# An encoder block on one core: five pairs of blocks by seven products, and accumulating transfers into the residual

## The chip, the cores and the metric

The kernel runs on one core of a Trainium2 chip. The metric is the device time of one execution in microseconds (us); the time before is 1480.17 us, the median of three runs (1477.66 to 1481.79). The core has a matrix engine (TensorE; PE in the profile, its weight loads PEld), a vector engine (DVE), a scalar engine (ACT), GpSimd (POOL) and a queue engine (SP). Each engine works through its own instructions in order; an instruction that waits for another engine or for a transfer holds up everything behind it on its engine. SBUF is the on-chip memory, PSUM holds what TensorE accumulates.

## The reference

One layer of an encoder, 256 tokens by 2048 features, all in 32-bit floats. In the names of the reference (`x` is the residual):

```python
h = rms_norm(x, attn_norm)
qa, ka, va, qb, kb, vb, ga, gb = split(h @ w_in)          # attention in two branches, with a bias table
ya, yb = windowed_gqa(qa, ka, va, ...), dilated_attention(qb, kb, vb, ...)
x = x + (sigmoid(ga) * (ya @ w_branch_a) + sigmoid(gb) * (yb @ w_branch_b)) @ w_out
hf = rms_norm(x, ffn_norm)
g = dwconv_centred(hf @ w_ffn_gate, conv_w, conv_b)
x = x + (gelu(g) * (hf @ w_ffn_up)) @ w_ffn_down          # 2048 -> 5632 -> 2048
x = x + sigmoid(rms_norm(x, ple_norm) @ w_ple_gate) * (p @ w_ple_proj)
return rms_norm(x, final_norm)
```

## The kernel before

**Weights.** All matrices stream through once, cut into 128x128 blocks; a piece is 16 blocks (1 MB), loaded by SP into one of three `raw` buffers (line 198), the next load being asked for when a buffer is free. Each matrix product is made of three 32-bit-rounded ones: a weight is split into a high part `whi` (ACT, line 217) and the rest `wlo` (DVE, line 218), an activation likewise; then high by high, high by low and low by high are added in PSUM. A split takes 8 blocks (1024 columns) as a rule. There are four buffers for splits (`bufs=4`), so that ACT can begin a split when TensorE has ended the one four before it.

**The list of jobs** (`_plan`, line 62) fixes the order: queries, keys and values with attention between them; the gates `ga`, `gb` and the branch products `ba`, `bb` for each quarter of the features; `o` (w_out); then twice 22 chunks of `g` and `u` (gate and up, half of the 44 feature chunks) followed by two down jobs (`d0`, then `d1`, each for the left and the right half of the 2048 output columns); then `pp` and `pg` (the embedding's projection and gate, four quarters each). Work that is due inside a job is hung on a step of it with `at((job, step), ...)`, and a scheduler makes each engine's final order of it.

**The down jobs** (`seven_product`, line 288) take 22 feature blocks as 11 pairs. A plain pair costs eight products of 128 tokens by 512 columns: `p2`, `p3`, `p4`, `c22` twice. A saved pair (numbers below `SAVED`, line 113) takes seven, after Strassen and Winograd: sums of weight blocks are made by DVE in `combine` (line 222: one subtraction of 1024 columns into a scratch tile, line 229, called t13 here; two of 512, lines 233 and 234), and the sums of activations have been made in `add_up` (line 704). A saved pair is split in four parts (1024, 1024, 1024 and 512 columns) that serve two, two, two and one products. `ORDER` (line 112) has the saved and the plain pairs take turns: 4 0 5 1 6 2 7 3 8 9 10. After the last saved pair `spread_sums` (line 721) adds the four extra sums `p1`, `p5`, `p6`, `p7` to the residual `res` with one ACT copy and eight DVE adds; at the end of the job `joined` (line 772) adds `p2`, `p3`, `p4`, `c22` with one DVE add each and, in `d1`, has ACT square the sum (line 781) for the next norm.

**Transposes.** `merge` (line 761) and `flip` (line 740) turn 256 features at a time with four TensorE transposes into a PSUM tile `pt` (two buffers); ACT and DVE then write both halves of the result (lines 367 and 368). In the right down job of `d1` the same two `pt` buffers hold `p6` and `p7`.

**The end.** `pg` multiplies, `gate` (line 783) makes the sigmoid, adds to the residual and has ACT square it; `finish` (line 795) sums the squares (line 798), takes the root on GpSimd (lines 387 and 389), scales and stores. The last gain is a 1 MB load (line 876) on ACT's queue.

Of the kernel before, what the change touches and what calls it, by code (L numbers as in the profile page):

```python
# [16 lines left out]
P = 128  # L17
# [94 lines left out]
ORDER = [4, 0, 5, 1, 6, 2, 7, 3, 8, 9, 10]  # L112
SAVED = 4
# [44 lines left out]
def _encoder(ctx: ExitStack, tc, xt, pt, cols, table, onehot, mask, ident_in, last_gain, wts, xrows, out):  # L158
# [63 lines left out]
    def combine(b, part):  # L222

        if part == 0:
            state["turn"] = turn = 1 - state.get("turn", 1)
            state["t"] = held["spare"][:, turn * PIECE * P:(turn + 1) * PIECE * P].rearrange("p (b n) -> p b n", n=P)
            four = b.rearrange("p (q b) n -> p q (b n)", q=4)
            t13 = state["t"][:, :8, :].rearrange("p (q b) n -> p q (b n)", q=2)
            nc.vector.tensor_tensor(t13, four[:, 1::2], four[:, :2], op=ALU.subtract)
            return b[:, 8:, :]  # L230
        if part == 1:
            t1, t2, t4 = (state["t"][:, c:c + 4, :] for c in (0, 8, 12))
            nc.vector.tensor_tensor(t2, b[:, 12:, :], t1, op=ALU.subtract)
            nc.vector.tensor_tensor(t4, b[:, 8:12, :], t2, op=ALU.subtract)
            return state["t"][:, :8, :]
        return state["t"][:, 8:, :] if part == 2 else b[:, :4, :]
# [200 lines left out]
    hba = big.tile([P, QH, AW], F32, name="hba", tag="b0", bufs=1)  # L437
    hbb = big.tile([P, BH, BW], F32, name="hbb", tag="b1", bufs=1)
# [62 lines left out]
    def bias(h0, n):  # L501

        if h0 < QH:
            dst, lines = hba[:, h0:h0 + n, :], [[1, P]]
# [25 lines left out]
    def scores(heads, y):  # L530
# [17 lines left out]
        a, step = (hba[:, h, :], P) if n == 1 else (hbb[:, h - QH, :], 1)  # L548
# [75 lines left out]
    def after(job, i, acc, u=None):  # L624
# [66 lines left out]
        elif kind == "u":  # L691
            u = gather(acc)
            nc.vector.scalar_tensor_tensor(u, u, 0.5, rt[1], op0=ALU.mult, op1=ALU.mult)
            f = n % FHALF
            v = held["a32"][:, f, :] if f < 2 * SAVED else u
            nc.vector.tensor_tensor(v, u, held.pop(("gelu", n)), op=ALU.mult)
            halves(held["act"][:, f, :], v)
            if f == 2 * SAVED - 1:
                add_up()
# [4 lines left out]
    def add_up():  # L704

        a = held["a32"].rearrange("p (m e) (t n) -> p m e t n", e=2, t=2)
        a11, a12, a21, a22 = a[:, :, 0, 0], a[:, :, 1, 0], a[:, :, 0, 1], a[:, :, 1, 1]
        s = held["s32"]
# [4 lines left out]
        hi, lo = held["shl"][:, 0], held["shl"][:, 1]  # L713
        for c in (slice(0, 2), slice(2, 4)):
            nc.scalar.activation(hi[:, c], s[:, c], AF.Copy)
            nc.vector.tensor_tensor(lo[:, c], s[:, c], hi[:, c].bitcast(F32), op=ALU.subtract)
# [3 lines left out]

    def spread_sums(n, bank):

        q = [[res[:, t, (2 * n + c) * W4:(2 * n + c + 1) * W4] for c in range(2)] for t in range(2)]
        u = held["ff"].tile([P, W4], F32, name="sq4")
        v = held["ff"].tile([P, W4], F32, name="gate", bufs=2)

        def add(dst, a, b):
            nc.vector.tensor_tensor(dst, a, b, op=ALU.add)

        nc.scalar.activation(u, bank["p1"], AF.Copy)  # L730
        add(q[0][0], u, q[0][0])
        add(u, bank["p6"], u)
        add(v, bank["p7"], u)
        add(u, bank["p5"], u)
        add(q[1][0], v, q[1][0])
        add(v, bank["p5"], v)
        add(q[0][1], u, q[0][1])
        add(q[1][1], v, q[1][1])
# [22 lines left out]
    def merge(n, e, m):  # L761
# [6 lines left out]
        hi, lo = (held["merged"][k // SUB][:, k % SUB:k % SUB + 2, c:c + T] for c in (0, T))  # L768
# [3 lines left out]
    def joined(n, t, acc, scale, parts):  # L772

        r = res[:, t, n * W4:(n + 1) * W4]
        if scale == 1.0:
            nc.vector.tensor_tensor(r, acc, r, op=ALU.add)
        else:
            nc.vector.scalar_tensor_tensor(r, acc, scale, r, op0=ALU.mult, op1=ALU.add)
        if parts is not None:
            q = held["ff"].tile([P, W4], F32, name="sq4")  # L780
            nc.scalar.activation(q, r, AF.Square, accum_out=parts[:, t, n:n + 1])

    def gate(n, t, acc, last):

        r = res[:, t, n * W4:(n + 1) * W4]
        u = held["ff"].tile([P, W4], F32, name="gate", bufs=2)
# [3 lines left out]
        q = held["ff"].tile([P, W4], F32, name="sq4")  # L790
        nc.scalar.activation(q, r, AF.Square, accum_out=held["ss3"][:, t, n:n + 1])  # L791
        nc.vector.tensor_tensor(u if last else r, r, held["lg"][:, n * W4:(n + 1) * W4], op=ALU.mult)
        return u

    def finish(t, tail):

        s = sc.tile([P, 2], F32, name="sum")[:, :1]
        nc.vector.tensor_reduce(s, held["ss3"][:, t, :], axis=AX.X, op=ALU.add)  # L798
        r = root(s, 1)
# [11 lines left out]
    def fetch(t, c):  # L811
# [9 lines left out]
        "o": lambda k: held["merged"][k // SUB][:, k % SUB, :], "ba": lambda k: yab[:, k, :],  # L821
# [5 lines left out]
    for i, job in enumerate(_JOBS):  # L827
# [4 lines left out]
        if kind == "gb" and n == 0:  # L832
            held["merged"] = [big.tile([P, SUB, 2 * T], FR, name="merged", tag=a, bufs=1) for a in ("b0", "b1")]
# [8 lines left out]
        if kind == "g" and n == 0:  # L842
            spare = held["spare"] = big.tile([P, KC * T], F32, name="spare", tag="b0", bufs=1)
            held["a32"] = spare[:, :2 * SAVED * T].rearrange("p (k t) -> p k t", t=T)
            held["s32"] = spare[:, 2 * SAVED * T:4 * SAVED * T].rearrange("p (e m n) -> p e m n", e=4, n=P)
# [3 lines left out]
        if kind == "d1" and n == 0:  # L849
            held["pl"] = big.tile([P, KC, 2 * T], FR, name="mov", bufs=1)  # L850
            pr = ff.tile([P, 2, T], F32, name="pr")
# [9 lines left out]
        if kind == "bb":  # L861
            for e in range(2):
                at((i + 1, 3 + 3 * e), merge, n, e, held["m"])
        if kind == "o":
            for e, j in enumerate(((i + 1, 2), (i + 1, 4)) if n < QUARTERS - 1 else ((i + 1, 9), (i + 1, 11))):
                at(j, flip, 4 * n + 2 * e, held["hf"], 1)
        if kind == "d1":
            for e, j in enumerate(((i + 2, 0), (i + 3, 0), (i + 3, 1), (i + 4, 1)) if n else
                                  [(i + 1, k) for k in (17, 18, 19, 20)]):
                at(j, flip, 8 * n + 2 * e, held["pl"], 2)  # L870
        if kind == "pp" and n == 0:
            end = ff.tile([P, 3 * QUARTERS, W4], F32, name="end", tag="act")
            held["ph"] = end[:, :2 * QUARTERS].rearrange("p (t n) w -> p t n w", t=2)
            held["lg"] = end[:, 2 * QUARTERS:].rearrange("p n w -> p (n w)")
        if kind == "pp" and n == 2:
# [47 lines left out]
        elif kind in ("d0", "d1"):  # L923
            for name, t, c in (("p2", 0, 0), ("p3", 0, 1), ("p4", 1, 0), ("c22", 1, 1)):
                joined(2 * n + c, t, acc[name], 1.0, held["ss2"] if kind == "d1" else None)
        elif kind == "pg":
            for t in range(2):
# [3 lines left out]
                if last:  # L931
                    finish(t, tail)
        else:
# [50 lines left out]
```

## Time and profile before

| | |
|---|---|
| runs before | 1481.79, 1480.17, 1477.66 us |
| profiled execution, its own time | 1477.88 us |
| span from the first to the last instruction | 1476.1 us |
| mean granted TensorE clock | 0.997 |
| DVE busy, ACT busy | 1065.5 us (72%), 760.5 us (52%) |
| all transfers | 282.88 MB, mean 192 GB/s; the weights' queue takes 50.8% of the DMA engines' time |

In a timeline row stand start, duration, engine, line, operation, `out<-in` by tile names, shape and count; in square brackets the idle time of the engine before it and who ended it. In rows of the view by lines stand count, busy time, mean duration in ns, idle time before. Matmuls overlap: the step from one start to the next is what one costs.

### The profile page before, as it was taken

To read this page: it belongs to the slowest core of one execution; us is meant where nothing else is said; L and a number is where in the kernel's file an instruction comes from. 1 tells how busy PE (TensorE), PEld (TensorE's weight loads), DVE (VectorE), ACT (ScalarE), POOL (GpSimd) and SP (SyncE) were. 2 spreads that over 40 slices of the span, in tenths; PEclk is the share of its full clock that TensorE was granted. 3 is DMA by queue.
4 is the path that set the end of the run, shared out by engine and by line. 5 is a ranking of instruction groups with operands and counts; after the bars stand their busy time and mean duration, and the time that the engine had idled before them with its cause. 6 is when DMAs were issued, how large, how long until landed. Compare 5 with 4: busy or idle time off the path is not lost. (4 is left out here: it accounts for less than half of the span.)

```text
span 1476.1 us, 19530 instructions
## 1 busy us (share of the span) xinstructions
PE 1462.2 (99%) x7570; PEld 1248.4 (85%) x7570; DVE 1065.5 (72%) x1530; ACT 760.5 (52%) x1072; POOL 3.7 (0%) x9
## 2 busy tenths in 40 slices
PE   9999999999999999999999999999999999999997
PEld 8888888888888888888888888888888888888886
DVE  7686664664554555568898888887889888898565
ACT  7465444444444444555555555554555555655643
POOL 0000000000000000000000000000000000000000
PEclk9999999999999999999999999999999999999998
DMA  9644444445555554545455454555455454555552
GB/s 321 245 156 171 169 171 171 171 177 194 204 197 192 202 207 180 198 171 197 178 196 196 180 196 171 205 223 192 183 196 189 184 198 172 201 200 216 211 188 97
DMA packets 46375, 282.88 MB, mean 192 GB/s; under 512 B 5124, under 2 KB 9988, under 8 KB 14028
## 3 DMA queue, kind: packets, MB, share of 16 engines
q1 hardware_dynamic: 44268, 277.31, 50.8%
q10 hardware_dynamic: 2016, 4.33, 1.1%
q8 instruction: 59, 0.97, 0.2%
q14 instruction: 32, 0.26, 0.0%
HBM read 279.49 MB, written 2.14 MB: 191 GB/s over the span
## 5 line engine op out<-in xcount | busy, mean ns | idle before, releaser
L218 DVE TENSOR_TENSOR wlo<-raw,whi 128x1024 fp32r<-128x1024 f32 (+2 forms) x519 | 622.1, 1201 | 355.6 <-ACT whi L217 352.4
L217 ACT ACTIVATE whi<-raw 128x1024 fp32r<-128x1024 f32 (+2 forms) x519 | 541.1, 1043 | 605.5 <-PE acc L269 224.9
L244 PE MATMUL acc<-mov,whi 128*128 128x512 f32 x1840 | 641.9, 393 | 0.3 <-DVE mov L368 0.3
L245 PE MATMUL acc<-mov,wlo 128*128 128x256 f32 x1840 | 512.8, 279 | 0.0
L244 PEld LDWEIGHTS acc<-mov,whi 128*128 128x128 f32 x1840 | 344.7, 187 | 77.6 <-DVE mov L368 0.6
L245 PEld LDWEIGHTS acc<-mov,wlo 128*128 128x128 f32 x1840 | 346.7, 188 | 0.4
L268 PE MATMUL acc<-wlo,mov 128*128 128x512 f32 (+1 forms) x512 | 196.5, 384 | 0.5 <-DVE wlo L218 0.5
L267 PE MATMUL acc<-whi,mov 128*128 128x512 f32 (+1 forms) x512 | 196.8, 385 | 0.0
L269 PE MATMUL acc<-whi,mov 128*128 128x512 f32 (+1 forms) x512 | 196.4, 384 | 0.0
L267 PEld LDWEIGHTS acc<-whi,mov 128*128 128x128 f32 x512 | 96.7, 189 | 19.3 <-DVE wlo L218 0.8
L268 PEld LDWEIGHTS acc<-wlo,mov 128*128 128x128 f32 x512 | 96.7, 189 | 19.0 <-DVE wlo L218 0.9
L269 PEld LDWEIGHTS acc<-whi,mov 128*128 128x128 f32 x512 | 96.7, 189 | 18.8
L312 PE MATMUL acc<-wlo,act 128*128 128x512 f32 x272 | 106.3, 391 | 0.8 <-DVE wlo L218 0.8
L311 PE MATMUL acc<-whi,act 128*128 128x512 f32 x272 | 106.1, 390 | 0.0
L313 PE MATMUL acc<-whi,act 128*128 128x512 f32 x272 | 105.9, 389 | 0.0
L312 PEld LDWEIGHTS acc<-wlo,act 128*128 128x128 f32 x272 | 51.1, 188 | 12.0 <-DVE wlo L218 1.7
L311 PEld LDWEIGHTS acc<-whi,act 128*128 128x128 f32 x272 | 51.1, 188 | 10.7
L313 PEld LDWEIGHTS acc<-whi,act 128*128 128x128 f32 x272 | 51.1, 188 | 10.5
L267 PE MATMUL acc<-whi,merged 128*128 128x512 f32 x128 | 50.6, 396 | 0.0
L269 PE MATMUL acc<-whi,merged 128*128 128x512 f32 x128 | 49.9, 390 | 0.0
L268 PE MATMUL acc<-wlo,merged 128*128 128x512 f32 x128 | 49.8, 389 | 0.0
L217 ACT ACTIVATE whi<-spare 128x1024 fp32r<-128x1024 f32 x32 | 33.7, 1054 | 27.0 <-PE acc L313 26.2
(177 smaller groups left out, 1373.0 us busy)
## 6 DMA issues: line engine op xcount, KB each, us to landing
raw<-in_wts SPq DMA_DIRECT2D x251, 1024.0 KB, 4.8
raw<-in_wts SPq DMA_DIRECT2D x12, 512.0 KB, 7.4
x<-in_xrows ACTq DMA_DIRECT2D x8, 256.0 KB, 5.3
x<-in_xt SPq DMA_DIRECT2D x13, 128.0 KB, 6.6
hbb<-hold SPq DMA_DIRECT2D x3, 514.0 KB, 6.3
hba<-hold SPq DMA_DIRECT2D x2, 768.0 KB, 7.1
end<-in_last_gain ACTq DMA_DIRECT2D x1, 1024.0 KB, 4.8
out<-x ACTq DMA_DIRECT2D x2, 384.0 KB
```

What stands on the lines that cost most here:

```text
L217: nc.scalar.activation(hi, src, AF.Copy)
L218: nc.vector.tensor_tensor(lo, src, hi.bitcast(F32), op=ALU.subtract)
L244: nc.tensor.matmul(acc, hi[:, o, :], m, start=first, stop=False, skip_group_check=True)
L245: nc.tensor.matmul(acc[:, T:], lo[:, o, :], m[:, :T], start=False, stop=last, skip_group_check=True)
L267: nc.tensor.matmul(acc, xh, hi, start=(k == 0), stop=False)
L268: nc.tensor.matmul(acc, xh, lo, start=False, stop=False)
L269: nc.tensor.matmul(acc, xl, hi, start=False, stop=(k == n - 1))
L311: nc.tensor.matmul(acc, xh, hi, start=(e == 1), stop=False)
L312: nc.tensor.matmul(acc, xh, lo, start=False, stop=False)
L313: nc.tensor.matmul(acc, xl, hi, start=False, stop=(e == uses[name]))
```

## The change

- `SAVED` goes from 4 to 5 and the order of pairs becomes 5 0 6 1 7 2 8 3 4 9 10: saved pairs 3 and 4 stand next to each other, and two plain pairs follow the last saved one.
- A ring of seven tiles `row` (128x512) in a new tag replaces `sq4`, `gate`, `pr` and the tiles of the saved activations (`two`, `s32`). The two scratch tiles of `combine` lie in separate places, and attention's table (`hba`, `hbb`) in two tags cut differently, so that SBUF holds it all.
- The sums of activations are made pair by pair (`add_up(m)`), not for all at once.
- `spread_sums` makes the four sums in rows (one ACT copy, four DVE adds) and sends each to the residual by a transfer on GpSimd's queue that adds to its destination (`to_residual`). The last four products of a down job are copied from PSUM to rows by ACT and sent likewise, except in the right job of `d1`, where `joined` still adds. The squares of the left job of `d1` are asked for at step 10 of the next job.
- `merge` and `flip` are hung on common steps, two at a time.
- The last gain is multiplied by the root of 2048 beforehand (DVE, 2048 columns), and most of the last sum of squares is made before the last quarter (`so_far`).

```diff
-ORDER = [4, 0, 5, 1, 6, 2, 7, 3, 8, 9, 10]
-SAVED = 4
+ORDER = [5, 0, 6, 1, 7, 2, 8, 3, 4, 9, 10]
+SAVED = 5
+SPLIT = 4
+ROWS = 7
...
-            state["t"] = held["spare"][:, turn * PIECE * P:(turn + 1) * PIECE * P].rearrange("p (b n) -> p b n", n=P)
+            t = state["t"] = held["spare"][turn]
...
+    hb0 = big.tile([P, GRP, AW], F32, name="hb0", tag="b0", bufs=1)
+    hb1 = big.tile([P, GRP * AW + BH * BW], F32, name="hb1", tag="b1", bufs=1)
...
+                if f % 2 == 0:
+                    held["two"] = ff.tile([P, 2, T], F32, name="two", tag="row", bufs=ROWS)
...
+            if f < 2 * SAVED and f % 2:
+                add_up(f // 2)
...
+    def row():
+        return held["ff"].tile([P, W4], F32, name="row", bufs=ROWS)
+
+    def to_residual(n, t, c, a):
+        keep(nc.gpsimd.dma_start(quarter(n, t, c), a, accum_op=ALU.add))
+
     def spread_sums(n, bank):
+        u = row()
         nc.scalar.activation(u, bank["p1"], AF.Copy)
-        add(q[0][0], u, q[0][0])
...
+        to_residual(n, 0, 0, u)
+        last = u
+        for name in ("p6", "p7"):
+            v = row()
+            nc.vector.tensor_tensor(v, bank[name], last, op=ALU.add)
+            last, u = v, last
+        u, v = u, last
+        to_residual(n, 1, 0, v)
+        w = row()
+        nc.vector.tensor_tensor(u, bank["p5"], u, op=ALU.add)
+        to_residual(n, 0, 1, u)
+        nc.vector.tensor_tensor(w, bank["p5"], v, op=ALU.add)
+        to_residual(n, 1, 1, w)
+
+    def squares_of(n, t, parts):
+        r = res[:, t, n * W4:(n + 1) * W4]
+        nc.scalar.activation(row(), r, AF.Square, accum_out=parts[:, t, n:n + 1])
...
+    def so_far():
+        e = held["early"] = sc.tile([P, 2], F32, name="sum")
+        nc.vector.tensor_reduce(e, held["ss3"][:, :, :QUARTERS - 1], axis=AX.X, op=ALU.add)
+        nc.vector.tensor_scalar(e, e, D * EPS, None, op0=ALU.add)
+
     def finish(t, tail):
-        nc.vector.tensor_reduce(s, held["ss3"][:, t, :], axis=AX.X, op=ALU.add)
-        r = root(s, 1)
+        nc.vector.tensor_tensor(v, held["ss3"][:, t, QUARTERS - 1:], held["early"][:, t:t + 1], op=ALU.add)
+        nc.gpsimd.tensor_tensor(r, v, mhalf[:, :1], op=ALU.pow)
...
-                at((i + 1, 3 + 3 * e), merge, n, e, held["m"])
+                at((i + 1, 4), merge, n, e, held["m"])
...
-            for e, j in enumerate(((i + 2, 0), (i + 3, 0), (i + 3, 1), (i + 4, 1)) if n else
-                                  [(i + 1, k) for k in (17, 18, 19, 20)]):
+            for e, j in enumerate([(i + 2, 0), (i + 2, 0), (i + 3, 1), (i + 3, 1)] if n else
+                                  [(i + 1, k) for k in (17, 17, 19, 19)]):
                 at(j, flip, 8 * n + 2 * e, held["pl"], 2)
...
+        if kind == "pp" and n == 3:
+            nc.vector.tensor_scalar(held["lg"], held["lg"], math.sqrt(D), None, op0=ALU.mult)
...
-                joined(2 * n + c, t, acc[name], 1.0, held["ss2"] if kind == "d1" else None)
+                if kind == "d1" and n:
+                    joined(2 * n + c, t, acc[name], 1.0, held["ss2"])
+                else:
+                    a = row()
+                    nc.scalar.activation(a, acc[name], AF.Copy)
+                    to_residual(n, t, c, a)
+                    if kind == "d1":
+                        at((i + 1, 10), squares_of, c, t, held["ss2"])
```

More of the change, by code (lines that the diff above doesn't have):

```diff
@@ L503, in bias @@
         if h0 < QH:
-            dst, lines = hba[:, h0:h0 + n, :], [[1, P]]
+            dst, lines = hba[h0 // GRP], [[1, P]]
         else:
@@ L702, in after, with add_up @@
                 nc.scalar.activation(held["ph"][:, t, n, :], acc[t], AF.Copy, scale=0.5)
[L704 to L708, printed above, removed]
+    def add_up(m):
+        (a11, a21), (a12, a22) = [[held["two"][:, e, h] for h in HALVES] for e in range(2)]
+        s = held["ff"].tile([P, 4, P], F32, name="s32", tag="row", bufs=ROWS)
         nc.vector.tensor_tensor(s[:, 0], a21, a22, op=ALU.add)
@@ L767, in merge @@
         k = 4 * n + 2 * e
-        hi, lo = (held["merged"][k // SUB][:, k % SUB:k % SUB + 2, c:c + T] for c in (0, T))
+        part, k = (held["merged"][k >= SPLIT], k - SPLIT * (k >= SPLIT))
+        hi, lo = (part[:, k:k + 2, c:c + T] for c in (0, T))
         nc.scalar.activation(hi, p, AF.Copy)
@@ L778, in joined @@
             nc.vector.scalar_tensor_tensor(r, acc, scale, r, op0=ALU.mult, op1=ALU.add)
-        if parts is not None:
-            q = held["ff"].tile([P, W4], F32, name="sq4")
-            nc.scalar.activation(q, r, AF.Square, accum_out=parts[:, t, n:n + 1])
+        squares_of(n, t, parts)
     def gate(n, t, acc, last):
         r = res[:, t, n * W4:(n + 1) * W4]
-        u = held["ff"].tile([P, W4], F32, name="gate", bufs=2)
+        u = row()
         nc.scalar.activation(u, acc, AF.Tanh, scale=held["half"][:, t:t + 1])
```

58 lines of the change are left out of this document (25 added, 33 removed).

## The prediction

> **What bounds the kernel now.** I read the page first (busy shares), then windows over the down jobs, then TensorE's timeline for every place where two matmuls start further apart than usual.
>
> ```profile
> PE 1462.2 (99%) x7570; PEld 1248.4 (85%) x7570; DVE 1065.5 (72%) x1530; ACT 760.5 (52%) x1072; POOL 3.7 (0%) x9
> ...
> 888.90:947.20 58.30, 57.87 (x256) 47.59 (x255) 50.93 (x58) 30.94 (x34) 0.00 (x0) 1.00 0.56 205
> 1251.00:1308.20 57.20, 57.20 (x254) 47.34 (x254) 50.70 (x58) 31.14 (x34) 0.00 (x0) 1.00 0.55 205
> ```
>
> TensorE is busy for 99% of the span; in a down job (the left ones of `d0` and `d1` are shown) DVE comes next, with 51 of 57 to 58 us, ACT with 31. So time is won only where matmuls go or TensorE stops waiting, and it is lost where DVE, ACT or a transfer becomes late. In the down jobs and at the start of `pg` TensorE waits in three places:
>
> ```profile
> 919.63 0.39 PE L311 MATMUL acc<-whi,act 128*128 128x512 f32 x1
> 920.45 0.50 PE L312 MATMUL acc<-wlo,act 128*128 128x512 f32 x1 [0.43 <-DVE wlo L218]
> ...
> 977.48 0.39 PE L311 MATMUL acc<-whi,act 128*128 128x512 f32 x1
> 978.25 0.50 PE L312 MATMUL acc<-wlo,act 128*128 128x512 f32 x1 [0.38 <-DVE wlo L218]
> ...
> 1381.10 0.39 PE L267 MATMUL acc<-whi,mov 128*128 128x512 f32 x1
> 1382.00 0.50 PE L268 MATMUL acc<-wlo,mov 128*128 128x512 f32 x1 [0.52 <-DVE wlo L218]
> ```
>
> The usual step from start to start is 0.227 us (a third of the 0.68 below). These are 0.82, 0.77 and 0.90: 0.59, 0.54 and 0.67 us lost, 1.8 in all. More than that cannot be won from waits.
>
> **The change part by part.**
>
> *The fifth pair.* A saved pair spares one product of three matmuls in each of four down jobs.
>
> ```profile
> 1342.42 0.39 PE L311 MATMUL acc<-whi,shl 128*128 128x512 f32 x1
> ...
> 1343.10 0.39 PE L311 MATMUL acc<-whi,act 128*128 128x512 f32 x1
> ```
>
> One product is 0.68 us, so 4 x 0.68 = **-2.72 us**; TensorE needs 7 x 0.68 = 4.76 us for a saved pair and 5.44 for a plain one. Its price on DVE:
>
> ```profile
> L218 DVE TENSOR_TENSOR wlo<-raw,whi 128x1024 fp32r<-128x1024 f32 x498 | 608.2, 1223 | 347.2 <-ACT whi L217 344.2
> L217 ACT ACTIVATE whi<-raw 128x1024 fp32r<-128x1024 f32 x498 | 528.4, 1061 | 581.0 <-PE acc L269 224.9 <-PE acc L244 176.1 <-issue 116.7
> L229 DVE TENSOR_TENSOR spare<-raw 128x1024 f32<-128x1024 f32 x16 | 19.5, 1221 | 4.1 <-DMA raw<-in_wts 3.9
> L218 DVE TENSOR_TENSOR wlo<-raw,whi 128x512 fp32r<-128x512 f32 x18 | 12.4, 688 | 5.1 <-ACT whi L217 5.0
> L234 DVE TENSOR_TENSOR spare<-raw,spare 128x512 f32<-128x512 f32 x16 | 11.0, 689 | 0.3
> L776 DVE TENSOR_TENSOR x<-acc,x 128x512 f32<-128x512 f32 x16 | 10.1, 684 | 1.8 <-PE acc L313 1.8
> L728 DVE TENSOR_TENSOR sq<-acc,sq 128x512 f32<-128x512 f32 x8 | 5.5, 686 | 0.1
> L730 ACT ACTIVATE sq<-acc 128x512 f32<-128x512 f32 x4 | 2.3, 581 | 0.0
> ```
>
> Three splits of 1.22, one of 0.69, a t13 of 1.22 and two subtractions of 0.69 are 6.95 us, against 2.45 for a plain pair: +4.5 a job. Four of the eight adds in `spread_sums` go (-2.74), and in three jobs the four of `joined` (-2.74). DVE's 51 us thus become 50, in the last job (49.2 in the right one of `d1`) about 51, of 57. Over a whole job DVE does not become the bound; the transfers buy room, not time. ACT takes over four copies of 0.58 us, with 26 us free.
>
> *Two saved pairs side by side* (3, 4) need 13.9 us of DVE in 9.5 us of TensorE. I walked this through with the durations above, from TensorE's start on plain pair 8 as zero (the same place before is 920.5). There four splits are done ahead, the last at 3.3. In the built order DVE then does t13 of pair 4 (to 4.5), the third split of 3 (5.7), both subtractions (7.1), its fourth (7.8), then the splits of 4, for which ACT waits until TensorE frees a buffer: ready at 9.1, 10.5, 11.9 and 12.6. TensorE needs them at 10.2, 11.6, 12.9 and 14.3. The lead of about 1 us hides it: **0**. The piece of pair 4 itself may be late, as here:
>
> ```profile
> 916.10 1.23 DVE L229 TENSOR_TENSOR spare<-raw 128x1024 f32<-128x1024 f32 x1 [1.44 <-DMA raw<-in_wts]
> ```
>
> 1.4 us late costs 0.1, each further us about one in each of four jobs.
>
> *Transposes in common.* Four transposes cost 0.35 us, and the matmul behind them 0.32 instead of 0.23:
>
> ```profile
> 1371.50 0.60 PE L745 MATMUL pt<-ident,x 128*128 128x128 f32 x4
> 1371.85 0.48 PE L267 MATMUL acc<-whi,pw 128*128 128x512 f32 x1
> 1372.17 0.40 PE L268 MATMUL acc<-wlo,pw 128*128 128x512 f32 x1
> ```
>
> In the built order 27 groups stand where 36 did: 9 x 0.09 = **-0.8**. But in the right job of `d1` the first four flips now stand 11 matmuls (2.5 us) after the last saved pair and need `pt`, which holds `p6` until DVE has added it. By the same walk that add ends 2.3 us after the pair, the one of `p7` 0.3 before its turn. If one split (1.22) comes between, TensorE waits 1.1, and once more for `p7`. Bounds 0 and 2.2; **+0.5**, near the lower, since the walk hides it.
>
> *Squares behind transfers.* The built order has ACT take the squares of the left half of `d1` not at step 10 but at the end J of its job: four copies, the second split of the next job's first saved pair, two squares, its third split, two squares, its fourth. A square now waits until the transfer has added that quarter, and every split behind it waits too. Before, the squares ran at once:
>
> ```profile
> 1306.60 1.06 ACT L217 ACTIVATE whi<-spare 128x1024 fp32r<-128x1024 f32 x1 [1.71 <-PE acc L313]
> 1307.56 0.62 ACT L781 ACTIVATE sq<-x 128x512 f32<-128x512 f32 x1
> ...
> 1309.69 1.05 ACT L217 ACTIVATE whi<-spare 128x1024 fp32r<-128x1024 f32 x1
> ```
>
> The trace has no adding transfer. The nearest rows, by size to landing:
>
> ```profile
> raw<-in_wts SPq DMA_DIRECT2D x12, 512.0 KB, 7.4
> x<-in_xrows ACTq DMA_DIRECT2D x8, 256.0 KB, 5.3
> end<-in_last_gain ACTq DMA_DIRECT2D x1, 1024.0 KB, 4.8
> out<-gate SPq DMA_DIRECT2D x2, 256.0 KB, 2.5
> ```
>
> The first copy ends at J-1.1, the others 0.6 us apart. At 5.3 us the sums land at J+4.2, 4.8, 5.4 and 6.0. The squares (0.76 us each) and splits follow: third split ready J+8.0 (needed J+8.2), fourth J+9.7 (9.7), then plain pair 6's first at J+11.2 (10.4). TensorE waits **+0.8**. At 2.5 it is 0, at 7.4 it is 2.9. I take 0.8, by the row of the same size. If the four run one after the other (J+4.2, 9.5, 14.8, 20.1) it is 13.3. The Trainium skill, "DMA: Bandwidth & Descriptors", section "Anatomy of one DMA — SWDGE (gpsimd) path", fits 2.0 us plus bytes over 436 GB/s to such transfers, by which an estimate for 256 KB is 2.6 us and this term 0; the row of 256 KB says 5.3, and no run here shows an adding one. Against the change speaks "SBUF — State Buffer", section "Who interferes with whom": GpSimd is blocked while DVE holds the ports that they share, which would delay the issue of a transfer; no row here shows it.
>
> *Joining the right half.* The adds of `joined` wait for the four earlier transfers; their last issue is about 6 us before the job's end, and the flips that need them come 2.7 us later, so landings up to 8 us cost nothing.
>
> *Start of `pg`.* In the built order TensorE no longer asks for the third split of `pg` early: **-0.7**. DVE has a new scaling of the gain there, which waits for its 1 MB. By
>
> ```profile
> L806 DVE TENSOR_SCALAR x<-x,rr 128x768 f32<-128x768 f32 x2 | 1.2, 612 | 0.0
> L802 DVE TENSOR_SCALAR gate<-gate,rr 128x512 f32<-128x512 f32 x2 | 1.0, 487 | 1.5 <-POOL rr L389 1.5
> ```
>
> (0.49 ns a column) it takes 1.24 us. With a landing of 4.8 us it ends about 0.5 us into `pg`, the split behind it 1.2 later, and TensorE needs that at 2.7: 0, with 1 us to spare.
>
> *The end.* One reduction leaves the last chain:
>
> ```profile
> 1469.41 0.16 DVE L798 TENSOR_REDUCE sum<-marks 128x1 f32<-128x4 f32 x1
> 1469.60 0.16 DVE L387 TENSOR_SCALAR rv<-sum 128x1 f32<-128x1 f32 x1
> ```
>
> One of two steps of 0.19: **-0.2**.
>
> *At nothing:* the sums of activations pair by pair and the embedding's load stand among `g` and `u`, where TensorE never waits and the next split is always more than one ahead; attention's table only lies elsewhere.
>
> **Sum:** -2.72 - 0.8 - 0.7 - 0.2 + 0.5 + 0.8 = -3.1 us. The profiled execution took 1477.88, so 1474.8; it lies 2.3 below the median of the runs, 1480.17, to which I apply the same difference: **1477.1**. The waits at 920 and 978 stay, since the pieces concerned are loaded in the same order.
>
> **The rivals.** Differences of more than 0.3% (4.4 us) are what a measurement of this kernel can tell: below 1475.7 and above 1484.6.
>
> *Everything hides.* The transfers land within 3 us (the row of 2.5 us is for it, the one of 5.3 against) and the flips find `pt` free: -4.4, and the 1.1 us of the waits at 920 and 978 may go too: -4.4 to -5.5, 1475.8 to 1474.7.
>
> *Adjacent pairs starve.* The piece of pair 4 comes 3 us late instead of 1.4. The order of loads is for it (its buffer is freed only by the last split of pair 2); the 1 us lead, and that only 3.9 us in sixteen t13 were waited, against. From 1.4 us lateness on TensorE pays all: 1.6 + 0.1 a job, 6.8: 1483.9.
>
> *Slower: adding transfers queue behind each other.* Each reads its destination as well, on engines that the weights already take for half of the time. It decides at the left job of `d1`, from a spacing of 2 us on (3.4 us lost there), and with full serialisation costs 13.3, and about 3 more where `joined` waits for its fourth landing. With the other terms, -4.4 + 0.5: between -0.5 and +12.4, I take +8: 1488.
>
> *The transfers do not do what they are for:* they take work from an engine that isn't the bound. That is within my forecast, and is why it has no gain of its own.
>
> **How the numbers follow.** Forecast 0.54 (its own range 1475.5 to 1481), everything hides 0.14, starving pairs 0.12, queued transfers 0.2. Faster: all of the second but 0.03, and 0.04 of the forecast: 0.15. Slower: 0.17 of the queued, 0.05 of the starving, 0.05 of the forecast for waits that I priced at nothing: 0.27. Within 0.3%: 0.58. Range 1474 to 1487: it takes in the first three cases and the cheaper half of the fourth.
>
> **What would show it.** After: 12 fewer matmuls on lines of `seven_product`; no TensorE wait on `wlo` in pair 4; ACT idle before the squares of `d1`'s left half with a transfer as releaser, and whether TensorE waits within 12 us behind it; no wait at the second split of `pg`; the transfers' time to landing and their spacing. I am wrong if TensorE waits at the flips or in `joined`, or if the landings are beyond 8 us.

## The result, and the profile after

The changed kernel takes 1490.76 us (median of 6 runs, 1489.57 to 1493.73), the kernel before 1479.85 (6 runs, 1477.66 to 1481.79). The ratio is 1.0078, with a 95% interval of 1.0064 to 1.0092: 10.9 us slower, where 1477.1 (1474 to 1487) was predicted. The profiled execution took 1491.17 us; its page begins so (below the span: busy us, share of the span, and count of instructions of each engine):

```profile
span 1489.4 us, 19654 instructions
...
PE 1467.2 (99%) x7558; PEld 1250.5 (84%) x7558; DVE 1072.7 (72%) x1561; ACT 774.2 (52%) x1098; POOL 28.5 (2%) x37
```

The twelve matmuls are gone (7558 for 7570). Yet TensorE is counted as busy for 5 us longer, so part of the loss is matmuls that ran slowly and not only waits. The busy shares show nothing else. What helps is TensorE's timeline, read for places where two starts lie further apart than the usual 0.227 us (below, the lost time is what a step takes beyond that). There are three kinds.

**The boundary between the jobs of `d1`.** TensorE's timeline of the changed kernel (start, duration, and in brackets the idle time and its releaser):

```profile
1315.98 0.39 PE L315 MATMUL acc<-whi,shl 128*128 128x512 f32 x1
1320.56 0.50 PE L313 MATMUL acc<-whi,shl 128*128 128x512 f32 x1 [4.19 <-ACT whi L219]
1321.82 0.79 PE L314 MATMUL acc<-wlo,shl 128*128 128x512 f32 x1 [0.76 <-DVE wlo L220]
1322.41 0.63 PE L315 MATMUL acc<-whi,shl 128*128 128x512 f32 x1
1322.83 0.63 PE L313 MATMUL acc<-whi,act 128*128 128x512 f32 x1
```

The first two steps lose 4.35 and 1.03 us. Behind them a matmul starts every 0.427 us, not every 0.227, up to 1327.95: another 3.0 us, 8.4 in all. Windows over the same place tell why (the columns are the stretch, its length, the busy us of PE, PEld, DVE, ACT and POOL, the granted TensorE clock, the DMA share, GB/s):

```profile
1305.00:1321.00 16.00, 11.81 (x52) 9.26 (x50) 7.52 (x8) 7.07 (x13) 4.39 (x5) 1.00 0.94 219
1321.00:1328.00 7.00, 6.24 (x16) 4.83 (x16) 6.92 (x8) 5.26 (x9) 0.00 (x0) 0.51 0.45 156
1385.50:1390.00 4.50, 4.21 (x16) 3.66 (x17) 2.13 (x6) 2.76 (x7) 0.00 (x0) 0.62 0.63 262
```

The granted clock is 1.00 before the wait and 0.51 for 7 us behind it (the last row belongs to the second place, below). What TensorE waited for is the split `whi<-tb`, and ACT's timeline shows what stood ahead of it:

```profile
1306.49 2.35 ACT L955 ACTIVATE row<-acc 128x512 f32<-128x512 f32 x4
1308.74 1.05 ACT L219 ACTIVATE whi<-tb 128x1024 fp32r<-128x1024 f32 x1
1317.59 0.63 ACT L757 ACTIVATE row<-x 128x512 f32<-128x512 f32 x1 [7.80 <-issue]
...
1319.46 1.04 ACT L219 ACTIVATE whi<-tb 128x1024 fp32r<-128x1024 f32 x1
...
1321.51 0.63 ACT L757 ACTIVATE row<-x 128x512 f32<-128x512 f32 x1 [0.39 <-DMA x<-row]
```

The four copies (L955) are done at 1308.8 and the second split at 1309.8. Then the first square (L757) holds ACT for 7.8 us. The reason named is "issue", which means that the view found no releaser; GpSimd's timeline has it. It shows the issues of the eight adding transfers of that job, the four of `spread_sums` and the four of the copies:

```profile
1298.64 0.87 POOL L735 DMA_DIRECT2D x<-row  x1 [280.56 <-ACT row L740]
1301.74 0.87 POOL L735 DMA_DIRECT2D x<-row  x1 [2.24 <-DVE row L745]
1303.48 0.90 POOL L735 DMA_DIRECT2D x<-row  x1 [0.86 <-DVE row L750]
1306.79 0.88 POOL L735 DMA_DIRECT2D x<-row  x1 [2.41 <-DVE tb L231]
1311.46 0.87 POOL L735 DMA_DIRECT2D x<-row  x1 [3.79 <-DMA x<-row]
1313.71 0.87 POOL L735 DMA_DIRECT2D x<-row  x1 [1.39 <-issue]
1316.57 0.90 POOL L735 DMA_DIRECT2D x<-row  x1 [1.98 <-DMA x<-row]
1317.83 0.88 POOL L735 DMA_DIRECT2D x<-row  x1 [0.37 <-issue]
```

The copy for the fifth transfer was done at 1307.1, its issue came at 1311.46. The trace has a landing time for each of the eight; worked out beside the issues they are:

| transfer | issued | landed | us to landing | issued after the landing of the third before it |
|---|---|---|---|---|
| 1 | 1298.64 | 1306.48 | 7.8 | |
| 2 | 1301.74 | 1311.14 | 9.4 | |
| 3 | 1303.48 | 1313.08 | 9.6 | |
| 4 | 1306.79 | 1316.25 | 9.5 | 0.31 |
| 5 | 1311.46 | 1317.52 | 6.1 | 0.32 |
| 6 | 1313.71 | 1318.76 | 5.0 | 0.63 |
| 7 | 1316.57 | 1320.05 | 3.5 | 0.32 |
| 8 | 1317.83 | 1321.42 | 3.6 | 0.31 |

From the fourth on, each issue comes 0.3 or 0.6 us after the landing of the third transfer before it. So there are never more than three in flight. The same holds in all four jobs of this run, for all 28 transfers. The first square could not start before the fifth had landed (1317.52), and it starts at 1317.59.

A second rule stands beside this one, and the program makes it: a transfer to a quarter waits until the transfer before it to the same quarter has landed. The fifth had that behind it (its quarter is that of the first, landed at 1306.48); the sixth, seventh and eighth follow the third, the second and the fourth.

**In `pp`.** DVE's timeline in the changed kernel, then TensorE's:

```profile
1376.38 1.29 DVE L796 TENSOR_TENSOR x<-acc,x 128x512 f32<-128x512 f32 x2 [1.07 <-DMA x<-row]
1379.89 0.69 DVE L796 TENSOR_TENSOR x<-acc,x 128x512 f32<-128x512 f32 x1 [2.22 <-DMA x<-row]
```

```profile
1385.79 1.70 PE L764 MATMUL pt<-ident,x 128*128 128x128 f32 x8 [2.03 <-DVE mov L370]
```

The adds of `joined` wait 3.3 us for the transfers of the same job. The squares, the split and the results of the flips behind them are late in turn, and TensorE loses 0.57 us at 1381, 2.19 at 1384 and, at a granted clock of 0.62, some 1.8 more: 4.6 in all.

**Late pieces.** In the down jobs four smaller losses (0.44, 0.33, 1.36 and 1.67 us) stand behind a `t13` that waited for its weights. DVE's idle time before everything that reads `raw`, from 880 to 1385 us, was put down to the weights for 17.2 us in nine places; in the kernel before for 3.9 us in five. The view's line for the kernel before, then for the changed one:

```profile
  DMA raw<-in_wts: 3.9, 5
```

```profile
  DMA raw<-in_wts: 17.2, 9
```

The page's rows on the transfers: the queue that carries them (packets, MB, share of 16 engines), and the issues (KB each, median us to landing):

```profile
q0 software_dynamic: 4032, 7.34, 2.8%
...
x<-row POOLq DMA_DIRECT2D x28, 256.0 KB, 8.2
...
x<-in_xrows ACTq DMA_DIRECT2D x8, 256.0 KB, 5.2
```

Together TensorE loses 8.4 + 4.6 + 3.8 = 16.8 us in the changed kernel where it lost 1.8 before. Less the twelve matmuls (2.7) that makes 12.3 more, between the 10.9 of the medians and the 13.3 of the two spans. Most of the remaining 1.0 is steps of 0.30 to 0.40 us in the down jobs, too short to be counted above.

### The profile page after: what moved, and what is told of

Its sections match the earlier page's. It is cut to its first block, busy times and chain, and to the rows that moved or that the text cites. A ratio compares the mean times of both kernels' runs of the same rounds, so it can differ in the third digit from the quotient of the medians.

```text
span 1489.4 us, 19654 instructions
## 1 busy us (share of the span) xinstructions
PE 1467.2 (99%) x7558; PEld 1250.5 (84%) x7558; DVE 1072.7 (72%) x1561; ACT 774.2 (52%) x1098; POOL 28.5 (2%) x37
## 4 chain that ended last, share of the span: by engine, by line
PE 52%; issue 40%; DMA 4%; DVE 3%; ACT 1%; POOL 0%; POOLq 0%; DVEq 0%; ACTq 0%
PE acc L246 22%; PE acc L247 11%; PE acc L314 3%; PE acc L315 3%; PE acc L313 3%; PE acc L271 2%; PE acc L270 2%; PE acc L269 2%; DMA raw<-in_wts 2%; PE first L246 2%; DVE wlo L220 2%; DMA x<-row 2%; PE first L247 1%; ACT whi L219 0%; DVE ta L231 0%
## 5 line engine op out<-in xcount | busy, mean ns | idle before, releaser
L314 PE MATMUL acc<-wlo,act 128*128 128x512 f32 x252 | 99.9, 396 | 3.1 <-DVE wlo L220 3.1
L315 PE MATMUL acc<-whi,act 128*128 128x512 f32 x252 | 99.4, 394 | 0.0
L313 PE MATMUL acc<-whi,act 128*128 128x512 f32 x252 | 99.1, 393 | 0.0
L314 PEld LDWEIGHTS acc<-wlo,act 128*128 128x128 f32 x252 | 47.9, 190 | 15.6 <-DVE wlo L220 5.8
L313 PEld LDWEIGHTS acc<-whi,act 128*128 128x128 f32 x252 | 48.0, 191 | 10.2
L315 PEld LDWEIGHTS acc<-whi,act 128*128 128x128 f32 x252 | 47.9, 190 | 9.7
L353 ACT ACTIVATE t<-acc 128x256 f32<-128x256 f32 x115 | 42.0, 365 | 0.0
```

The lines of the kernel that those rows point to most:

```text
L313: nc.tensor.matmul(acc, xh, hi, start=(e == 1), stop=False)
L314: nc.tensor.matmul(acc, xh, lo, start=False, stop=False)
L315: nc.tensor.matmul(acc, xl, hi, start=False, stop=(e == uses[name]))
L353: keep(nc.scalar.activation(t, acc[:, T:], AF.Copy, scale=scale))
```

## The experiments

All are edits of the changed kernel; e8, e14 and e15 leave sums out of the residual. Each time is a median; the ratio to the kernel before, run beside it on the same chip, stands with its 95% interval.

| run | what differs from the changed kernel | us | ratio to before |
|---|---|---|---|
| e1_adds | DVE adds in place of all transfers | 1478.58 | 0.9995 [0.9986, 1.0005] |
| e2_late_squares | squares of `d1`'s left half later | 1486.11 | 1.0055 [1.0039, 1.0070] |
| e3_left_adds | last four of `d1`'s left job by DVE | 1488.67 | 1.0068 [1.0055, 1.0081] |
| e4_four_pairs | four saved pairs, with transfers | 1490.24 | 1.0077 [1.0064, 1.0090] |
| e5_spread_order | e1, saved pairs never adjacent | 1480.98 | 1.0014 [1.0006, 1.0023] |
| e6_late_gain | e1, gain scaled later | 1476.97 | 0.9984 [0.9976, 0.9993] |
| e7_d0_transfers | transfers in `d0` alone | 1482.08 | 1.0019 [1.0009, 1.0030] |
| e8_overwrite | transfers overwrite | 1482.24 | 1.0024 [1.0015, 1.0033] |
| e9_no_late_reader | e2, `spread_sums` of `d1`'s right job by DVE | 1486.32 | 1.0045 [1.0033, 1.0058] |
| e10_copied_first | e6, last four results of `d0` copied by ACT first | 1475.55 | 0.9973 [0.9963, 0.9984] |
| e11_flips_apart | e6, transposes where they were | 1478.82 | 0.9994 [0.9985, 1.0003] |
| e12_four_adds | e6, four saved pairs | 1476.90 | 0.9983 [0.9975, 0.9992] |
| e13_four_copied | e10, four saved pairs | 1478.44 | 0.9992 [0.9984, 1.0001] |
| e14_narrow | e9, an eighth of each transfer | 1478.59 | 1.0001 [0.9989, 1.0012] |
| e15_overwrite_no_late | e9, transfers overwrite | 1483.46 | 1.0032 [1.0020, 1.0044] |

**The transfers or the fifth pair?** Two runs part them. In e1:

```diff
-        keep(nc.gpsimd.dma_start(quarter(n, t, c), a, accum_op=ALU.add))
+        nc.vector.tensor_tensor(quarter(n, t, c), a, quarter(n, t, c), op=ALU.add)
...
-                if kind == "d1" and n:
-                    joined(2 * n + c, t, acc[name], 1.0, held["ss2"])
+                if True:
+                    joined(2 * n + c, t, acc[name], 1.0, held["ss2"] if kind == "d1" else None)
```

> No adding transfers: all results reach the residual by DVE adds, as before the change; five pairs in the new order, and all else of the change, stay. Theory (the loss lies in waits for the transfers: about 8.7 us at the boundary of the two jobs of d1, about 4 us at the start of pp, some of 3.8 us of late pieces): 1475 to 1478 us, 2 to 5 us faster than before the change, no TensorE wait over 1 us at the boundary of d1 or at pp. Rival (two saved pairs side by side, and five of them, starve TensorE by late pieces): 1483 us or more, with the waits at the saved pairs still there.

In e4:

```diff
-ORDER = [5, 0, 6, 1, 7, 2, 8, 3, 4, 9, 10]
-SAVED = 5
+ORDER = [4, 0, 5, 1, 6, 2, 7, 3, 8, 9, 10]
+SAVED = 4
```

> Four saved pairs in the order of before, with all else of the change. Theory (the loss comes from the transfers): 12 more matmuls, so 1490 to 1494 us, the waits at the boundary and at pp as in the changed kernel. Rival (the fifth pair, side by side with the fourth, is what costs): 1484 us or less.

e4's time came out as the theory has it, 1490.24, with 3.5 us lost at the same square and a slow clock behind it. The wait expected in `pp` isn't in its trace; late pieces cost 6.6 us there instead of 3.8. Without transfers the loss is gone: e1 is level with the kernel before. But it is only level, just above what was expected. Its timelines show what ate the gain. TensorE's rows at the three places:

```profile
1003.32 0.47 PE L246 MATMUL acc<-mov,whi 128*128 128x512 f32 x1 [0.89 <-DVE x L796]
...
1280.68 0.50 PE L314 MATMUL acc<-wlo,act 128*128 128x512 f32 x1 [1.50 <-DVE wlo L220]
...
1380.04 0.47 PE L269 MATMUL acc<-whi,mov 128*128 128x512 f32 x1 [1.82 <-DVE mov L370]
```

and DVE's rows ahead of the last of them:

```profile
1378.27 1.23 DVE L901 TENSOR_SCALAR end<-end 128x2048 f32<-128x2048 f32 x1 [2.05 <-DMA end<-in_last_gain]
1379.41 0.87 DVE L370 SCALAR_TENSOR_TENSOR mov<-pt,cl,mov 128x256 fp32r<-128x256 f32 x2
```

The time lost is 1.05 us for a bank that DVE frees with its add, 1.67 for a late piece, and 1.98 at the start of `pg`, because the scaling of the gain waits for its 1 MB with the results of the flips queued behind it. The sum is 4.7 us.

**The squares.** e2 holds the squares of the left half at a later step:

```diff
-                        at((i + 1, 10), squares_of, c, t, held["ss2"])
+                        at((i + 1, 14), late_squares, c, t, held["ss2"])
...
+    def late_squares(n, t, parts):
+        r = res[:, t, n * W4:(n + 1) * W4]
+        keep(nc.scalar.activation(row(), r, AF.Square, accum_out=parts[:, t, n:n + 1]))
```

> Only the squares of the left half of d1 are moved: held at step 14 of the next job instead of at the end of their own. Theory (ACT stands at the squares until a transfer has landed, and the splits queued behind it are late): the 8.7 us at the boundary go, 1481 to 1484 us; the loss at the start of pp stays. Rival (the transfers are slow for all, so the wait only moves to the next reader): 1488 us or more, with a wait of the same size within 20 us behind the squares.

It took 1486.11, between the two. The wait of 4.35 us and the slow clock behind it are gone, and no wait of that size follows. In their place stand 1.2 us at a split nearby and several late pieces in `d0` and `d1`. So the squares were what held TensorE there, but by the times less than half of the 10.9 us went with them. Late pieces also vary from one execution to the next: in `d0`, ahead of the edit, this trace loses 4.9 us at them and that of the changed kernel 2.1, with the same instructions in the same order.

**Adds in the left job.** In e3 the condition of the copies becomes

```diff
-                if kind == "d1" and n:
+                if kind == "d1":
```

> Only in the left job of d1 the last four results are added by DVE and squared at once; spread_sums still uses transfers there. Theory (four copies, four transfers and the squares behind them are what costs at the boundary): 1481 to 1484 us, as with late squares; the loss at pp stays. Rival (the four transfers of spread_sums are late too, and the adds, which write the same quarters, wait for them on DVE): 1486 us or more, with DVE idle at the adds until a transfer has landed.

The rival holds. DVE now waits for the transfers of `spread_sums`, which bring the other part of the same quarters, and TensorE loses 3.5 us at 1318 with a slow clock behind it. DVE's row of e3:

```profile
1318.29 2.01 DVE L796 TENSOR_TENSOR x<-acc,x 128x512 f32<-128x512 f32 x3 [6.00 <-DMA x<-row]
```

So the rule on a quarter holds for DVE as well: its add waits until the transfer to that quarter has landed.

**Is a transfer that nobody waits for free?** In e7 only `d0` has them:

```diff
-        keep(nc.gpsimd.dma_start(quarter(n, t, c), a, accum_op=ALU.add))
...
+        if n_job[0] == "d0":
+            keep(nc.gpsimd.dma_start(quarter(n, t, c), a, accum_op=ALU.add))
+        else:
+            nc.vector.tensor_tensor(quarter(n, t, c), a, quarter(n, t, c), op=ALU.add)
```

> Adding transfers in the two jobs of d0 alone (16 of 28), where no instruction reads the sums for over 100 us; d1 adds by DVE. Theory (transfers also make weights' pieces late, for they share the DMA engines): late pieces in d0 cost 2 to 5 us against DVE adds everywhere, 1480 to 1484 us. Rival (transfers cost only where an instruction waits for their sums): 1478.5 us or less, since DVE has less to do and the 1.05 us lost at 1002 behind an add go.

It is not. e7 lies 3.1 us above e1 (2.7 above its kernel before, against 0.5 below), and what it loses more is lost at late pieces. DVE's wait for weights in the view shown above, for e1 and then for e7:

```profile
  DMA raw<-in_wts: 3.6, 3
```

```profile
  DMA raw<-in_wts: 13.0, 7
```

The copies by ACT, which e7 has in `d0` and e1 lacks, are not the cause: e10 below has them without transfers, and there the same line says 3.7 us. The loads themselves are longer. From the issues and landings in the traces: ten of e7's loads of weights were under way together with a transfer, and they took 6.7 us on average; the same ten loads took 4.9 in e1. In the changed kernel it is 17 loads, with 6.7 us for 4.9 in e1.

e9 takes away the last reader as well, on top of e2:

```diff
-        keep(nc.gpsimd.dma_start(quarter(n, t, c), a, accum_op=ALU.add))
...
+        if n_job[0] == ("d1", 1):
+            nc.vector.tensor_tensor(quarter(n, t, c), a, quarter(n, t, c), op=ALU.add)
+        else:
+            keep(nc.gpsimd.dma_start(quarter(n, t, c), a, accum_op=ALU.add))
```

> Late squares as in e2, and the four results of the last right job's spread_sums are added by DVE, so that no instruction near the end reads a quarter right behind a transfer; 24 of 28 transfers stay. Theory (what is then left of the loss is the late weights, 3 to 5 us against DVE adds everywhere): 1481 to 1484 us, and less than 2 us lost at the start of pp. Rival (the loss at pp has another cause, such as the flips or the gain): 1485 us or more, with over 3 us lost there.

Its time is what the rival said, above the theory's, and by the medians it is no faster than e2 (7.7 us above its kernel before, e2 7.1). The wait in `pp` is gone, as the theory said, but now TensorE loses 2.06 us at the start of `pg` to the scaling of the gain, as in e1. The larger part is late weights: 9.1 us of TensorE's time at steps over 0.4 us in the down jobs, nearly all at late pieces and splits, where e1 has 1.9.

**What of a transfer makes weights late?** e8 and e15 leave out `accum_op`; e14 narrows the transfer (the edit is against e9):

```diff
-            keep(nc.gpsimd.dma_start(quarter(n, t, c), a, accum_op=ALU.add))
+            keep(nc.gpsimd.dma_start(quarter(n, t, c)[:, :W4 // 8], a[:, :W4 // 8], accum_op=ALU.add))
```

> The 28 transfers overwrite the residual instead of adding to it, with the same bytes, places and waits; the sums are left out, so the output is not the reference's. Theory (the path and the load beside it set the 8.2 us to landing, not the adding): landings of 6.5 to 9 us, 1487 to 1492 us. Rival (reading the destination and adding is what takes the time): landings of 5.3 us or less, as for the plain load of 256 KB, and 1484 us or less.

> As e9, but the 24 transfers overwrite instead of adding; the sums are left out, so the output is not the reference's. Theory (late weights follow the time that transfers take on the DMA engines, 1.2% of the engines' span instead of 2.8% for 28 of them): the 7.7 us shrink to about 3.3, 1481 to 1483 us. Rival (they follow the bytes or the packets' places, not the adding): 1485 us or more.

> As e9, but each of the 24 transfers carries only 64 of its 512 columns; the rest of these sums is left out, so the output is not the reference's. Theory (the weights are late because the transfers take time on the DMA engines for their bytes): the 7.7 us between e9 and DVE adds shrink to 1 to 2.5, 1479 to 1481.5 us, and DVE's waits for weights in the down jobs fall from 19 us to under 8. Rival (a transfer costs by its packets and its queue, whatever it carries): 1484 us or more, with those waits over 14 us.

In e8 the rival nearly holds: by the time, and but for 0.2 us by the landings. A transfer that overwrites lands in 5.5 us, close to the plain load's 5.2, and 8 of the 10.9 us are gone: the adding costs. Page rows of e8:

```profile
q0 software_dynamic: 2240, 7.34, 1.2%
...
x<-row POOLq DMA_DIRECT2D x28, 256.0 KB, 5.5
```

For the same bytes an adding transfer has 144 packets instead of 80 and takes 2.3 times as long on the DMA engines (2.8% of the engines' span for 1.2%). Up to four overwriting transfers were in flight, three adding ones, in every run. The waits for weights of DVE, and the rows of the queue, for e9, e15 and e14 in turn:

```profile
  DMA raw<-in_wts: 19.3, 10
...
q0 software_dynamic: 3456, 6.29, 2.4%
```

```profile
  DMA raw<-in_wts: 18.0, 10
...
q0 software_dynamic: 1920, 6.29, 1.1%
```

```profile
  DMA raw<-in_wts: 9.2, 9
...
q0 software_dynamic: 3456, 0.79, 0.6%
```

TensorE's own losses, counted as for e9, are 9.1, 6.8 and 4.0 us: the same order as the queue's share, but not in proportion to it. Against their kernels before, the three runs lie at +7.7, +4.2 and -0.7. With an eighth of the bytes and all the packets no price is left that the times can show, so it isn't the count of transfers or packets alone. But overwriting, with less than half of the engines' time, still costs 4.7 us over e1, above the 1481 to 1483 expected; DVE waits almost as long, and in e14 somewhat longer than the 8 us expected. The loads of weights agree: those under way with a transfer took 6.5 us in e9, 6.4 in e15 and 5.1 in e14, where the same loads took 5.0 in e1. So the price comes with the bytes that move beside the weights. Whether it goes by the bytes themselves or by the time that they take on the engines isn't settled: the intervals of e9 and e15, which move the same bytes, overlap.

**What the remaining edits are worth.** e6 moves the scaling of the gain:

```diff
-        if kind == "pp" and n == 3:
-            nc.vector.tensor_scalar(held["lg"], held["lg"], math.sqrt(D), None, op0=ALU.mult)
+        if kind == "pg" and n == 0:
+            at((i, 8), lambda: keep(nc.vector.tensor_scalar(held["lg"], held["lg"], math.sqrt(D), None, op0=ALU.mult)))
```

> No adding transfers, five saved pairs in the changed order; the scaling of the gain by DVE is moved from the end of pp to step 8 of the first pg job. Theory (in the run with DVE adds this scaling waited 2.05 us for its 1 MB with the flips' results queued behind it, and TensorE lost 1.98 us at 1377.8): 1476 to 1477 us, and no wait over 1 us at that place. Rival (the flips that stand together are late anyway, by DVE's four adds ahead of them): 1478 us or more, the wait in the same place behind other work.

As expected: 2.0 us less than e1 against their kernels before, and 0.80 lost at that place for 1.98.

e5 spreads the saved pairs (`ORDER = [0, 5, 1, 6, 2, 7, 3, 8, 4, 9, 10]`, DVE adds):

> No adding transfers, five saved pairs, but the order of pairs is 0, 5, 1, 6, 2, 7, 3, 8, 4, 9, 10: no two saved pairs side by side, and a saved pair first. Theory (the one late piece that remains with DVE adds, 1.7 us at 1278.8, comes of the order): it goes, 1476 to 1477.5 us. Rival (five saved pairs strain DVE and the loads whatever their order, so the wait comes up at another piece): 1478 us or more, with a late piece elsewhere in the four jobs.

The rival holds. The piece at 1278 is in time, but TensorE now waits for banks behind three of the four jobs (0.9 to 1.05 us each) and at the first plain pair of each (0.5 to 0.7); the gain's scaling costs 2.6 here, with a slow clock behind it. The adjacent pairs are not what costs.

e10 lets ACT empty the banks in both jobs of `d0`, with DVE adding the copies. The expectation names the left job of `d1` too, but the kernel has `joined` in both jobs of `d1`:

```diff
-        keep(nc.gpsimd.dma_start(quarter(n, t, c), a, accum_op=ALU.add))
+        nc.vector.tensor_tensor(quarter(n, t, c), a, quarter(n, t, c), op=ALU.add)
...
-                if kind == "d1" and n:
+                if kind == "d1":
                     joined(2 * n + c, t, acc[name], 1.0, held["ss2"])
```

> DVE adds and the late gain of e6; the last four results of both jobs of d0 and of the left job of d1 are first copied out of their banks by ACT, and DVE adds the copies. Theory (the 1.05 us at 1002 of the run with DVE adds is TensorE waiting for a bank that DVE frees with its add): that wait goes, 1475.5 to 1476.5 us. Rival (DVE is late there for all that it does, so the wait moves to a split): 1477 us or more.

The wait at 1002 is gone and the time is in the range expected. This is the fastest kernel of the study: 3.1 us under the kernel before, 14.0 under the changed one by the two differences to before.

e12 is e6 and e13 is e10, each with the `ORDER` and `SAVED` of e4; e11 is e6 with the steps of the transposes of before.

> As e6, but four saved pairs in the order of before. Theory (the fifth pair is worth its twelve matmuls, 2.7 us, less what it adds in waits): 1478 to 1480 us. Rival (side by side with the fourth it gives its gain back on DVE and in late pieces): 1477 us or less.

> As e10, but four saved pairs in the order of before. Theory (in e6 the fifth pair's gain was eaten by the wait for a bank, which e10 took away, so that it now shows): 1477 to 1478.5 us. Rival (a fifth pair is worth nothing in any arrangement, since the pieces come no earlier): 1476 us or less.

> As e6, but the transposes stand where they stood before the change, in 36 groups instead of 27. Theory (common groups save 0.09 us each, 0.8 in all): 1477.5 to 1478 us. Rival (standing together they make DVE late at the start of pg, so that nothing is saved): 1476 to 1477 us.

With banks freed by adds the fifth pair is worth little (e6 against e12: 0.1 us more by the medians, 0.7 less against their kernels before). With banks freed by copies it is worth 2.9 us by the medians and 2.3 against the kernels before (e10 and e13), which is about its 2.72; the traces account for 1.0 of that, e6's wait at the bank, and the intervals of e10 and e13 just touch. The copies alone, with four pairs, don't help (e13 against e12), so by these times it is the two together. e11 is 1.9 us slower than e6, more than the 0.8 expected, but the two intervals overlap, and a late piece of 1.6 us in e11's trace, at a place where e6 has none, makes most of it; the transposes' own worth isn't settled to better than that.

## Why the prediction was wrong

**Squares behind transfers: the step that failed.** The prediction let each transfer start when its copy was done, put 5.3 us to landing, and got +0.8; the place was right. Measured were 8.4 us. The landings of the four themselves averaged 4.5 us, less than priced. Two things were missing ahead of them. At most three adding transfers are in flight, and the four of `spread_sums`, taking 7.8 to 9.6 us each, still held the queue when the copies were done, and three of the four quarters with it; so the fifth was issued 4.4 us late and the eighth 9. The change itself shows eight transfers to four quarters, two for each. The second thing is the clock: a price of 1 us per us of lateness misses the 3.0 us at half speed behind a wait this long.

**The slower rival is what came**, at the place it named; it took 1488 and got 0.2 of the chances. Its mechanism was half right. It had the four transfers of the copies run one behind the other, and put its point of decision at a spacing of 2 us. Those four landed only 1.3 us apart, with up to three in flight; what made them late is the four ahead of them. Over all eight the landings lie 2.1 us apart on average (from 1306.48 to 1321.42). What should have raised it is in the prediction's own text: the trace had no adding transfer, and the row used for one was a plain load's. e8 shows that this row was right for a plain transfer on that queue (5.5 against 5.3) and that adding costs another 2.7 us at the median. The Trainium skill, "DMA: Bandwidth & Descriptors", section "Anatomy of one DMA — SWDGE (gpsimd) path", gave an estimate of 2.6 us for 256 KB; beside the weights' loads these runs show 8.2 adding and 5.5 overwriting.

**`joined` in the right half: priced at nothing up to landings of 8 us.** The three landings that it waited for were 8.6 to 9.7 us, the last issue 4.8 us before the end of the job instead of 6, and TensorE lost 4.6 us. This was named as a way to be wrong.

**The loads of weights "in the same order": same order, later.** No term was kept for transfers that slow the loads. e7 prices it at 3.1 us for 16 transfers that nobody waits for. The waits at 920 and 978, said to stay, are late pieces of this kind: in the changed kernel's trace the first is gone and the second has grown to 1.36, and in others both, one or neither appear.

**The gain's scaling: priced at nothing with 1 us to spare.** Right in the changed kernel, where no wait stands at the start of `pg`, since TensorE was late there anyway; with that lateness gone it costs 1.98 us (e1). The load took 6.1 us in e1 instead of 4.8.

**The fifth pair: -2.72.** e10 and e13 fit it, e6 and e12 don't: with adds from the banks it was worth 0.7 at most. The prediction didn't see the wait of 1.0 us at a bank, which e6 has and e12, with four pairs, has not.

**Adjacent pairs: 0.** Right. No wait stood at the pair itself in the changed kernel, and spreading the pairs (e5) was slower than leaving them adjacent (e1).

**Flips that need `pt`: +0.5.** No wait; the lower bound, 0, was right. **Transposes -0.8, start of `pg` -0.7, last chain -0.2:** their sum of 1.7 fits the time of e12, which has them, four pairs and no transfers, and is 1.8 us faster than before. In the changed kernel's trace `pg` takes 86.8 us from its first to its last matmul for 87.7 before, and the step is gone from the last chain. The transposes' gain isn't seen: 16 groups of four stand as seven of eight and two of four ahead of the first down job, yet it starts at 888.97 us for 888.99 before.

## What to carry to other kernels

Before work is moved from an engine with room to a transfer, find what the transfer has to share: here the limit on transfers in flight, the destination that two of them add to, and the loads that feed the bound engine. Count every transfer that stands ahead of the one whose landing you price, and price an adding one from a run that has one. A change that saves matmuls in a job pays only if what frees that job's banks keeps up, so try it together with a faster way to empty them.

## What the hardware showed that was not expected

**Three in flight.** In all seven kernels with adding transfers (of 32 KB in e14, of 256 KB in the others), no transfer was issued while three before it had not landed; the next issue came 0.26 us or more after the landing. Transfers that overwrite reached four. As narrow ones obey the same limit, it isn't set by bytes; that it follows from the packets (144 for an adding transfer, 80 for an overwriting one) fits, but wasn't tried.

**The clock falls after a short wait.** Wherever two matmuls started 2.42 us or more apart late in the kernel (2.42 twice, 2.82, 2.85, 3.69, 3.70, 4.58), those behind ran at half speed for 3.4 us (five times) or 6.8 us (twice); after 2.18, 2.21, 2.24 and 2.29 us they didn't. Windows behind the wait of 2.82 us in e14 and behind the one of 2.21 us in e1:

```profile
1381.00:1385.00 4.00, 3.92 (x11) 3.13 (x12) 3.73 (x4) 0.17 (x1) 0.00 (x0) 0.62 0.25 88
```

```profile
1380.00:1384.00 4.00, 3.96 (x18) 3.32 (x19) 3.69 (x4) 1.65 (x2) 0.00 (x0) 1.00 0.31 100
```

In the same 4 us TensorE did 11 matmuls in the one and 18 in the other. The Trainium skill, "TensorE: Matmul & The Clock Gate", section "Part 1: The HAM clock gate (the "warmup" mystery)", has half rate follow an idle window of about 3.4 us; the half rate agrees, but here a step of 2.42 us from start to start, 2.03 of it idle by the profile, was enough.
